# Block sums of a weight tile written over its own blocks, and the scaling of x moved ahead of the weight splits in two engines' queues

## The chip, the cores and the metric

One Trainium2 chip; the kernel runs on one of its cores. The metric is the device time of one execution in microseconds (us). A matmul runs on PE (TensorE); DVE is VectorE, ACT is ScalarE, POOL is GpSimd, SP is the engine whose queue issues most DMAs.

## The reference, cut to what matters

A decoder layer on 256 rows of width 2048 in float32: a feed-forward block, a mixing layer, a second feed-forward block, a final norm. Both feed-forward blocks (hidden width 5632) compute

```python
def swiglu(x, w_gate, w_up, w_down):
    return (jax.nn.silu(x @ w_gate) * (x @ w_up)) @ w_down
h = h + 0.5 * swiglu(rms_norm(h, ffn1_norm[l]), ffn1_w_gate[l], ffn1_w_up[l], ffn1_w_down[l])
```

The change lies in `x @ w_gate` and `x @ w_up` of these two blocks.

## The kernel before, in words

**Split products.** Every float32 operand is held as a high part (fp32r, a CAST by ACT) and a low part (what the cast lost, a subtraction by DVE). A product is three matmuls: high times high, high times low, low times high (`three`, L133 to L138). A weight block can therefore not be used before ACT and then DVE have split it: `split` (L93 to L101, L99 on ACT, L100 on DVE) takes one buffer of tag `whi` and one of `wlo`, of which there are three each, and a buffer comes free when the last matmul that reads it is done.

**Chunks and passes.** The hidden width is cut in a first chunk of 512 columns and five of 1024 (`ffn`, L246 on). The first chunk uses ordinary products (`weights`, `rows_times`; its splits are L81 and L82). Each of the five others is a gate pass and an up pass (L315, L321), so there are 20 passes in the two blocks. A pass goes over eight pairs of 128-row weight tiles, in the order of the plan "nSnSnSnn": `n` is an ordinary pair (two splits of 128x1024, 24 matmuls), `S` is a pair done by a Strassen-like scheme (21 matmuls) on the four 128x512 blocks b11, b12 (upper row) and b21, b22. This text calls the three S pairs of a pass S1, S2 and S3.

**An S pair before the change** (`pairs`, L103 to L131). It needs b11 and b21 (one split of 128x1024), b22 (a split of 128x512), and four sums: t1 = b12 - b11 and t3 = b22 - b12 (L125, one instruction of 128x1024), t2 = t3 + b11 (L127), t4 = b21 - t2 (L128). The sums go to a second `wst` buffer (there are three `wst` buffers in all, 1 MB each, and a DMA from HBM fills one per pair), and are split in turn: t1 with t3, then t2 with t4. So an S pair has four splits: (b11, b21), b22, (t1, t3), (t2, t4). PE takes b21, b11, b22, then t1 and t3, t2, t4 (L156 to L162), and the pair before and after it are ordinary or S by the plan. The splits go round the three buffers, so the buffers of b22 and of (t1, t3) are those that the two halves of the ordinary pair before it gave up.

**What sets the order.** The program is not ordered by hand. A scheduler runs it once against a model when it is built, and each engine's queue is the order in which instructions start there: of those that are ready, the one with the smallest number starts, and that number is the place in the program less an offset. Loads, splits and sums of weights carry an offset of 4000 (L60, L111), all the rest, if nothing is said, none.

**After a pass.** At the last S the partial sums in PSUM are combined (`shared`, L300 to L304, DVE and ACT). After a gate pass DVE adds them to four banks (L317) and ACT takes silu (L318); after an up pass DVE adds and multiplies (L324, L325). The transposes of the hidden values and their split (`hidden_T`, L270 and L271) come at pair 6 of the next gate pass.

**Scaling of x.** The row scale of the norm is known late, so the first gate chunk runs on x without it. While the first up chunk runs, `normalised(p)` (L275 to L292) rescales x in place, pair p of its 16 tiles after PE has read that pair: L279 and L280 add the parts and multiply (DVE), L281 casts (ACT), L282 subtracts (DVE); for the three pairs that the S pairs use, four sums of x (L286 to L289), their cast (L291) and subtraction (L292) follow. The temporary is one for all p, so p + 1 follows p. The first gate pass starts with pair p = 3 (an ordinary one), then S1 with p = 0.

Of the kernel before, what the change touches and what calls it, by code (L numbers as in the profile page):

```python
# [12 lines left out]
F32 = mybir.dt.float32  # L13
F32R = mybir.dt.float32r
AF = mybir.ActivationFunctionType
ALU = mybir.AluOpType
PSUM = bass.MemoryType.PSUM
P = 128
# [3 lines left out]
class Core:  # L22
# [80 lines left out]
    def pairs(self, mat, c0, plan):  # L103


        nc = self.nc
        ns = plan.count("S")
        ids = {"S": iter(range(ns)), "n": iter(range(ns, self.NK // 2))}
        for kind in plan:
            p = next(ids[kind])  # L110
            with self.tc.high_priority(offset=4000):  # L111
                st = self.wpool.tile([P, 2 * self.WMAX], F32, name=self.name("wst"), tag="wst")
                nc.sync.dma_start(
                    out=st.rearrange("p (k f) -> p k f", k=2),
                    in_=mat[2 * p * P : (2 * p + 2) * P, c0 : c0 + 1024].rearrange("(k p) f -> p k f", p=P),
                )
                b = st.rearrange("p (k n f) -> p k n f", k=2, n=2)
                if kind == "n":
                    parts = [self.split(b[:, k], 2) for k in range(2)]
                else:  # L120
                    b11, b21 = self.split(b[:, :, 0, :], 2)
                    (b22,) = self.split(b[:, 1, 1:2, :], 1)
                    tt = self.wpool.tile([P, 2 * self.WMAX], F32, name=self.name("wst"), tag="wst")
                    t = tt.rearrange("p (n f) -> p n f", f=512)
                    nc.vector.tensor_tensor(t[:, 0:2], b[:, :, 1, :], b[:, 0], ALU.subtract)  # L125
                    t1, t3 = self.split(t[:, 0:2], 2)
                    nc.vector.tensor_tensor(t[:, 2], t[:, 1], b[:, 0, 0, :], ALU.add)  # L127
                    nc.vector.tensor_tensor(t[:, 3], b[:, 1, 0, :], t[:, 2], ALU.subtract)  # L128
                    t2, t4 = self.split(t[:, 2:4], 2)
                    parts = dict(b11=b11, b21=b21, b22=b22, t1=t1, t2=t2, t3=t3, t4=t4)  # L130
            yield kind, p, parts  # L131

# [113 lines left out]
def ffn(core, xhi, xlo, rstd, wg, wu, wd, after_first, after_down, fpool, down, rest, back, head=None):  # L246
    nc, NT, NK, D, S = core.nc, core.NT, core.NK, core.D, core.S
# [10 lines left out]
    def hidden_T(c0, w, hid):  # L258
        for j in range(0, w // P, 2):
            bk = core.bank(4 + j // 2)  # L260
            for jj in range(2):
                for t in range(NT):
                    nc.tensor.transpose(  # L263
                        bk[:, jj * 256 + t * P : jj * 256 + (t + 1) * P],
                        hid[:, t, (j + jj) * P : (j + jj + 1) * P],
                        core.ident,
                    )
            k = c0 // P + j
            dst = hT_hi[:, k : k + 2, :].rearrange("p k s -> p (k s)")
            nc.scalar.copy(dst, bk)  # L270
            nc.vector.tensor_tensor(  # L271
                hT_lo[:, k : k + 2, :].rearrange("p k s -> p (k s)"), bk, dst.bitcast(F32), ALU.subtract
            )

    def normalised(p):  # L275

        pair = slice(2 * p, 2 * p + 2)
        tmp = scrap[:, 0, 512:].rearrange("p (k s) -> p k s", k=2)
        nc.vector.tensor_tensor(tmp, xhi[:, pair, :].bitcast(F32), xlo[:, pair, :].bitcast(F32), ALU.add)  # L279
        nc.vector.tensor_tensor(tmp, tmp, core.rb[:, None, :].to_broadcast([P, 2, S]), ALU.mult)  # L280
        nc.scalar.copy(xhi[:, pair, :], tmp)  # L281
        nc.vector.tensor_tensor(xlo[:, pair, :], tmp, xhi[:, pair, :].bitcast(F32), ALU.subtract)  # L282
        if p < NSUM:
            blk = lambda k, t: tmp[:, k, t * P : (t + 1) * P]
            raw = scrap[:, 1, 512:].rearrange("p (n s) -> p n s", n=4)
            nc.vector.tensor_tensor(raw[:, 0], blk(0, 1), blk(1, 1), ALU.add)  # L286
            nc.vector.tensor_tensor(raw[:, 1], raw[:, 0], blk(0, 0), ALU.subtract)
            nc.vector.tensor_tensor(raw[:, 2], blk(0, 0), blk(0, 1), ALU.subtract)
            nc.vector.tensor_tensor(raw[:, 3], blk(1, 0), raw[:, 1], ALU.subtract)  # L289
            flat = raw.rearrange("p n s -> p (n s)")  # L290
            nc.scalar.copy(sums[:, p, 0, :], flat)  # L291
            nc.vector.tensor_tensor(sums[:, p, 1, :], flat, sums[:, p, 0, :].bitcast(F32), ALU.subtract)  # L292

    def blocks_of(dst):
        return [dst[:, t, n * 512 : n * 512 + 512] for t in range(NT) for n in range(2)]

    def shared(aux, dst):

        d11, d12, d21, d22 = blocks_of(dst)
        nc.scalar.copy(d11, aux[0])  # L300
        nc.vector.tensor_tensor(d21, aux[2], d11, ALU.add)
        nc.vector.tensor_tensor(d12, aux[1], d21, ALU.add)
        nc.vector.tensor_tensor(d21, aux[3], d21, ALU.add)
        nc.vector.tensor_tensor(d22, aux[1], d21, ALU.add)  # L304
# [3 lines left out]
    for c0, w in chunks:  # L308
        if c0:
            own, aux = ([core.bank(i) for i in b] for b in (range(4), range(4, 8)))  # L310
            sg = fpool.tile([P, NT, 1024], F32, name=core.name("sg"), tag="sg")
            last_s = GATE_PLAN.rindex("S")
            hooks = {last_s: [lambda: shared(aux, sg)]}
            hooks.setdefault(HIDDEN_AT, []).extend(pending)
            core.rows_times_pairs(wg, c0, GATE_PLAN, own, aux, xhi, xlo, sums, hooks)  # L315
            for d, bk in zip(blocks_of(sg), own):
                nc.vector.tensor_tensor(d, bk, d, ALU.add)  # L317
                core.last_silu = nc.scalar.activation(d, d, AF.Silu)  # L318
            own, aux = ([core.bank(i) for i in b] for b in (range(4, 8), range(4)))
            hid = fpool.tile([P, NT, 1024], F32, name=core.name("hid"), tag="hid")  # L320
            core.rows_times_pairs(wu, c0, UP_PLAN, own, aux, xhi, xlo, sums,  # L321
                                  {UP_PLAN.rindex("S"): [lambda: shared(aux, hid)]})
            for d, g, bk in zip(blocks_of(hid), blocks_of(sg), own):
                nc.vector.tensor_tensor(d, bk, d, ALU.add)  # L324
                nc.vector.tensor_tensor(d, d, g, ALU.mult)  # L325
            pending = [lambda c0=c0, w=w, hid=hid: hidden_T(c0, w, hid)]
            continue
        nb = (w + 511) // 512
        cuts = [(n, n * 512, min(512, w - n * 512)) for n in range(nb)]
        gb = [[core.bank(t * nb + n) for n in range(nb)] for t in range(NT)]  # L330
        for i, (k, hi, lo) in enumerate(core.weights([(wg, c0, w)], ks, head=bool(head))):
            core.rows_times(gb, xhi, xlo, k, hi, lo, w, i == 0, i == NK - 1)
            if head and i in head:
                with core.tc.high_priority(offset=3000), core.tc.issue_after(core.last_mm.ins):
                    head[i]()
        after_first()
        sg = fpool.tile([P, NT, 1024], F32, name=core.name("sg"), tag="sg")
        for t in range(NT):
            for n, c, ww in cuts:
                core.last_silu = nc.scalar.activation(sg[:, t, c : c + ww], gb[t][n][:, :ww], AF.Silu, scale=rstd[:, t : t + 1])  # L340
        ub = [[core.bank(4 + t * nb + n) for n in range(nb)] for t in range(NT)]
        for i, (k, hi, lo) in enumerate(core.weights([(wu, c0, w)], ks)):
            core.rows_times(ub, xhi, xlo, k, hi, lo, w, i == 0, i == NK - 1)
            if i == 0:
                sums, scrap = rest(), sg
            if i % 2:
                normalised(i // 2)
        hid = fpool.tile([P, NT, 1024], F32, name=core.name("hid"), tag="hid")
        for t in range(NT):
            for n, c, ww in cuts:  # L350
                nc.vector.scalar_tensor_tensor(  # L351
                    hid[:, t, c : c + ww], ub[t][n][:, :ww], rstd[:, t : t + 1], sg[:, t, c : c + ww],
                    ALU.mult, ALU.mult,
                )
        pending = [lambda c0=c0, w=w, hid=hid: hidden_T(c0, w, hid)]
# [853 lines left out]
```

## Time and profile before

| | us |
|---|---|
| median of 3 runs (lowest to highest) | 1953.48 (1951.44 to 1953.81) |
| the profiled execution, its own time | 1948.99 |
| its span in the profile | 1947.3 |
| PE busy in the span | 1907.3 (98%) |
| DVE busy | 1440.3 (74%) |
| ACT busy | 985.8 (51%) |
| mean granted clock of PE (1 is full) | 0.994 |

The span is the time from the first to the last instruction that the profile shows. Matmuls are pipelined, and one that takes 0.39 us starts 0.23 us behind the one before it, so a wait of PE of under some 0.16 us does not show in its busy time: PE's waits are read from single rows.

### The profile page before, as it was taken

The page shows a single profiled execution, that of the slowest core. Times are in us where ns is not written, and L with a number is a line of the kernel's source. Part 1 is how long each engine was busy: PE and PEld are TensorE (multiplying, and loading weights), DVE is VectorE, ACT ScalarE, POOL GpSimd, SP SyncE. Part 2 cuts the span into 40 slices and gives each one's busy share as a digit, 9 for nine tenths or more (in the row PEclk, how much of TensorE's full clock was granted, in tenths as well). Part 3 has the DMA queues.
Part 4 walks back from the last instruction along what each step waited for, and adds up shares of the span by engine and source line. Part 5 has one row for each costly group of instructions (what it writes and reads, how often), then busy time and mean ns, then how long its engine had stood idle before and what let it go on. Part 6 is the DMA issues. An engine that isn't in the chain of part 4 may idle for free.

```text
span 1947.3 us, 25669 instructions
## 1 busy us (share of the span) xinstructions
PE 1907.3 (98%) x10233; PEld 1589.7 (82%) x10233; DVE 1440.3 (74%) x1822; ACT 985.8 (51%) x1189; POOL 9.9 (1%) x53
## 2 busy tenths in 40 slices
PE   8899999999999999999999999999999999999997
PEld 6678877878888889998899878778888888788886
DVE  5989898888645446876696775899898989844553
ACT  6465555555444335544454555565556555543443
POOL 0000000000000001000000000000000000000000
PEclk9999999999999999999999999999999999999999
DMA  6356555565755556545243456555555655766553
GB/s 238 129 198 214 173 194 195 178 212 190 264 186 204 194 195 207 177 127 163 77 144 115 131 195 215 173 194 182 199 197 198 211 183 184 257 211 193 195 194 129
DMA packets 130032, 360.77 MB, mean 185 GB/s; under 512 B 20879, under 2 KB 23128, under 8 KB 129784
## 3 DMA queue, kind: packets, MB, share of 16 engines
q1 hardware_dynamic: 129592, 358.08, 55.6%
q8 instruction: 80, 1.31, 0.3%
q10 hardware_dynamic: 320, 1.06, 0.1%
q14 instruction: 40, 0.33, 0.0%
HBM read 351.25 MB, written 7.86 MB: 184 GB/s over the span
## 4 chain that ended last, share of the span: by engine, by line
PE 89%; DVE 5%; ACT 3%; issue 2%; DMA 1%; SPq 0%; ACTq 0%; DVEq 0%
PE bank L137 14%; PE bank L136 13%; PE bank L138 13%; PE bank L175 10%; PE bank L177 10%; PE bank L174 10%; PE bank L186 4%; PE bank L188 4%; PE bank L187 4%; ACT whi L99 1%; DVE wlo L82 1%; PE bank L263 1%; DVE wlo L100 1%; PE bank L712 1%; PE bank L640 1%
## 5 line engine op out<-in xcount | busy, mean ns | idle before, releaser
L82 DVE TENSOR_TENSOR wlo<-wst,whi 128x1024 fp32r<-128x1024 f32 (+2 forms) x329 | 398.2, 1212 | 344.6 <-ACT whi L81 343.9
L99 ACT CAST whi<-wst 128x1024 fp32r<-128x1024 f32 (+1 forms) x440 | 430.4, 993 | 364.0 <-PE bank L138 321.9
L81 ACT CAST whi<-wst 128x1024 fp32r<-128x1024 f32 (+2 forms) x329 | 343.2, 1044 | 472.5 <-PE bank L177 335.8
L100 DVE TENSOR_TENSOR wlo<-wst,whi 128x1024 fp32r<-128x1024 f32 (+1 forms) x440 | 493.3, 1147 | 90.9 <-ACT whi L99 85.0
L174 PE MATMUL bank<-whi,hThi 128*128 128x512 f32 x704 | 274.2, 389 | 0.0
L175 PE MATMUL bank<-wlo,hThi 128*128 128x512 f32 x704 | 274.0, 389 | 0.0
L177 PE MATMUL bank<-whi,hTlo 128*128 128x512 f32 x704 | 231.4, 389 | 0.0
L186 PE MATMUL bank<-xahi,whi 128*128 128x256 f32 x688 | 199.1, 290 | 3.2 <-DVE raw L571 3.2
L188 PE MATMUL bank<-xahi,wlo 128*128 128x256 f32 x688 | 197.9, 288 | 0.0
L136 PE MATMUL bank<-whi,xahi 128*128 128x512 f32 x490 | 191.4, 393 | 6.3 <-ACT xahi L281 4.6
L187 PE MATMUL bank<-xalo,whi 128*128 128x256 f32 x688 | 197.3, 287 | 0.0
L137 PE MATMUL bank<-wlo,xahi 128*128 128x512 f32 x490 | 191.5, 391 | 0.6 <-DVE wlo L100 0.6
L136 PE MATMUL bank<-whi,xbhi 128*128 128x512 f32 x490 | 190.2, 391 | 1.9 <-DVE hid L351 1.4
L137 PE MATMUL bank<-wlo,xbhi 128*128 128x512 f32 x490 | 191.1, 390 | 0.6 <-DVE wlo L100 0.6
L138 PE MATMUL bank<-whi,xalo 128*128 128x512 f32 x490 | 191.4, 391 | 0.0
L138 PE MATMUL bank<-whi,xblo 128*128 128x512 f32 x490 | 190.7, 389 | 0.0
L175 PEld LDWEIGHTS bank<-wlo,hThi 128*128 128x128 f32 x704 | 132.2, 188 | 27.4
L177 PEld LDWEIGHTS bank<-whi,hTlo 128*128 128x128 f32 x704 | 132.1, 188 | 27.4
L174 PEld LDWEIGHTS bank<-whi,hThi 128*128 128x128 f32 x704 | 132.2, 188 | 27.1
L186 PEld LDWEIGHTS bank<-xahi,whi 128*128 128x128 f32 x688 | 133.1, 193 | 7.3 <-DVE raw L571 3.6
L188 PEld LDWEIGHTS bank<-xahi,wlo 128*128 128x128 f32 x688 | 132.9, 193 | 1.9 <-issue 1.1
L187 PEld LDWEIGHTS bank<-xalo,whi 128*128 128x128 f32 x688 | 133.1, 194 | 1.2 <-issue 0.2
(298 smaller groups left out, 2557.3 us busy)
## 6 DMA issues: line engine op xcount, KB each, us to landing
wst<-in_ffn_w_up_dram SPq DMA_DIRECT2D x88, 1024.0 KB, 5.0
wst<-in_ffn_w_down_dram SPq DMA_DIRECT2D x88, 1024.0 KB, 4.9
wst<-in_ffn_w_gate_dram SPq DMA_DIRECT2D x87, 1024.0 KB, 5.0
wst<-in_w_in_dram SPq DMA_DIRECT2D x40, 1024.0 KB, 5.0
wst<-in_w_out_dram SPq DMA_DIRECT2D x16, 1024.0 KB, 5.7
h<-parked SPq DMA_DIRECT2D x4, 1024.0 KB, 9.2
wst<-in_w_in_dram SPq DMA_DIRECT2D x4, 640.0 KB, 4.4
h<-in_x_dram SPq DMA_DIRECT2D x4, 512.0 KB, 4.7
```

Of the source, the lines that this page charges most:

```text
L82: nc.vector.tensor_tensor(lo[:, : m * width], src, hi[:, : m * width].bitcast(F32), ALU.subtract)
L99: self.nc.scalar.copy(hv, src)
L100: self.nc.vector.tensor_tensor(lv, src, hv.bitcast(F32), ALU.subtract)
L136: nc.tensor.matmul(out, a[0], b[0], start=first, stop=False)
L137: nc.tensor.matmul(out, a[0], b[1], start=False, stop=False)
L138: self.last_mm = nc.tensor.matmul(out, a[1], b[0], start=False, stop=last)
L174: nc.tensor.matmul(banks[t][n][:, :w], a, whi[:, c : c + w], start=first, stop=False)
L175: nc.tensor.matmul(banks[t][n][:, :w], a, wlo[:, c : c + w], start=False, stop=False)
L177: self.last_mm = nc.tensor.matmul(banks[t][n][:, :w], b, whi[:, c : c + w], start=False, stop=last)
L186: nc.tensor.matmul(out, a, xhi[:, k, :], start=first, stop=False, skip_group_check=True)
L187: nc.tensor.matmul(out, a, xlo[:, k, :], start=False, stop=False, skip_group_check=True)
L188: nc.tensor.matmul(out, b, xhi[:, k, :], start=False, stop=last, skip_group_check=True)
```

## The change

In `pairs`, the second `wst` buffer goes. The four sums are written over the blocks of the loaded tile: w22 becomes t3, w12 becomes t1, w11 becomes t2, w21 becomes t4, by four instructions of 128x512. A block is overwritten, so its split and every other reader come first. The splits of (t1, t3) and (t2, t4) then read the loaded tile. In `ffn`, `normalised` runs under an offset of 4500.

```diff
                     b11, b21 = self.split(b[:, :, 0, :], 2)
                     (b22,) = self.split(b[:, 1, 1:2, :], 1)
-                    tt = self.wpool.tile([P, 2 * self.WMAX], F32, name=self.name("wst"), tag="wst")
-                    t = tt.rearrange("p (n f) -> p n f", f=512)
-                    nc.vector.tensor_tensor(t[:, 0:2], b[:, :, 1, :], b[:, 0], ALU.subtract)
-                    t1, t3 = self.split(t[:, 0:2], 2)
-                    nc.vector.tensor_tensor(t[:, 2], t[:, 1], b[:, 0, 0, :], ALU.add)
-                    nc.vector.tensor_tensor(t[:, 3], b[:, 1, 0, :], t[:, 2], ALU.subtract)
-                    t2, t4 = self.split(t[:, 2:4], 2)
+
+                    w11, w12, w21, w22 = b[:, 0, 0, :], b[:, 0, 1, :], b[:, 1, 0, :], b[:, 1, 1, :]
+                    nc.vector.tensor_tensor(w22, w22, w12, ALU.subtract)
+                    nc.vector.tensor_tensor(w12, w12, w11, ALU.subtract)
+                    nc.vector.tensor_tensor(w11, w22, w11, ALU.add)
+                    nc.vector.tensor_tensor(w21, w21, w11, ALU.subtract)
+                    t1, t3 = self.split(b[:, :, 1, :], 2)
+                    t2, t4 = self.split(b[:, :, 0, :], 2)
                     parts = dict(b11=b11, b21=b21, b22=b22, t1=t1, t2=t2, t3=t3, t4=t4)
...
             if i % 2:
-                normalised(i // 2)
+                with core.tc.high_priority(offset=4500):
+                    normalised(i // 2)
```

## Rows read from the trace of the kernel before

**Rows 1.** The page: busy time of the engines; the chain that ended last, by engine.

```profile
PE 1907.3 (98%) x10233; PEld 1589.7 (82%) x10233; DVE 1440.3 (74%) x1822; ACT 985.8 (51%) x1189; POOL 9.9 (1%) x53
...
PE 89%; DVE 5%; ACT 3%; issue 2%; DMA 1%; SPq 0%; ACTq 0%; DVEq 0%
```

**Rows 2.** Who waited for whom, whole span: us in total, times, longest us.

```profile
PEld bank L137 <- DVE wlo L100: 18.7, 54, 0.9
...
ACT whi L99 <- DMA wst<-in_ffn_w_gate_dram: 10.0, 13, 1.6
```

**Rows 3.** Timeline at an S2, PE's weight load: start us, us, instruction, idle before.

```profile
316.76 0.19 PEld L137 LDWEIGHTS bank<-wlo,xsums 128*128 128x128 f32 x1 [0.38 <-DVE wlo L100]
```

**Rows 4.** Timeline of ACT at the same S2: casts of b22 and (t1, t3).

```profile
311.63 0.63 ACT L99 CAST whi<-wst 128x512 fp32r<-128x512 f32 x1 [1.64 <-PE bank L138]
314.40 1.05 ACT L99 CAST whi<-wst 128x1024 fp32r<-128x1024 f32 x1 [2.14 <-PE bank L138]
```

**Rows 5.** Timeline of DVE at the same S2: low part of b22, last sum, low part of (t1, t3).

```profile
312.68 0.68 DVE L100 TENSOR_TENSOR wlo<-wst,whi 128x512 fp32r<-128x512 f32 x1
313.28 0.68 DVE L128 TENSOR_TENSOR wst<-wst,wst 128x512 f32<-128x512 f32 x1
315.48 3.72 DVE L100 TENSOR_TENSOR wlo<-wst,whi 128x1024 fp32r<-128x1024 f32 x3 [1.52 <-ACT whi L99]
```

**Rows 6.** Timeline of DVE in the first block's scaling: each waits for the one before.

```profile
69.36 0.69 DVE L282 TENSOR_TENSOR xalo<-sg,xahi 128x512 fp32r<-128x512 f32 x1 [0.68 <-ACT xahi L281]
70.08 0.69 DVE L279 TENSOR_TENSOR sg<-xahi,xalo 128x512 f32<-128x512 f32 x1
70.81 0.69 DVE L280 TENSOR_TENSOR sg<-sg,rb 128x512 f32<-128x512 f32 x1
```

**Rows 7.** Timeline of DVE and ACT between a gate pass and its up pass's S1.

```profile
378.42 1.28 DVE L317 TENSOR_TENSOR sg<-bank,sg 128x512 f32<-128x512 f32 x2
381.34 3.50 DVE L100 TENSOR_TENSOR wlo<-wst,whi 128x1024 fp32r<-128x1024 f32 x3 [1.64 <-ACT whi L99]
...
379.14 1.23 ACT L318 ACTIVATE sg<-sg 128x512 f32<-128x512 f32 x2 [0.78 <-DVE sg L317]
380.28 2.97 ACT L99 CAST whi<-wst 128x1024 fp32r<-128x1024 f32 x3
```

**Rows 8.** Timeline of DVE between an up pass and the next gate pass's S1.

```profile
327.07 1.22 DVE L125 TENSOR_TENSOR wst<-wst 128x1024 f32<-128x1024 f32 x1
328.24 0.69 DVE L324 TENSOR_TENSOR hid<-bank,hid 128x512 f32<-128x512 f32 x1
...
329.98 0.69 DVE L127 TENSOR_TENSOR wst<-wst,wst 128x512 f32<-128x512 f32 x1
...
333.66 0.69 DVE L100 TENSOR_TENSOR wlo<-wst,whi 128x512 fp32r<-128x512 f32 x1
334.27 0.69 DVE L325 TENSOR_TENSOR hid<-hid,sg 128x512 f32<-128x512 f32 x1
334.87 1.28 DVE L324 TENSOR_TENSOR hid<-bank,hid 128x512 f32<-128x512 f32 x2
336.07 1.28 DVE L325 TENSOR_TENSOR hid<-hid,sg 128x512 f32<-128x512 f32 x2
337.27 3.49 DVE L100 TENSOR_TENSOR wlo<-wst,whi 128x1024 fp32r<-128x1024 f32 x3
```

**Rows 9.** Timeline of PE at the first block's first gate pass.

```profile
69.38 0.80 PE L136 MATMUL bank<-whi,xahi 128*128 128x512 f32 x1 [4.56 <-ACT xahi L281]
```

**Rows 10.** Windows: us, busy PE, PEld, DVE, ACT, POOL (instructions), granted clock, DMA, GB/s.

```profile
60.00:70.00 10.00, 3.18 (x11) 1.76 (x10) 9.28 (x16) 3.19 (x5) 0.00 (x0) 0.77 0.33 105
70.00:80.00 10.00, 9.79 (x38) 7.47 (x37) 8.53 (x13) 5.20 (x7) 0.00 (x0) 0.89 0.32 105
...
1250.00:1260.00 10.00, 8.64 (x39) 6.82 (x38) 10.00 (x16) 5.21 (x6) 0.00 (x0) 1.00 0.25 85
1260.00:1270.00 10.00, 8.88 (x35) 6.33 (x35) 8.47 (x13) 4.07 (x6) 0.00 (x0) 1.00 0.44 144
```

## The prediction, made before the changed kernel was seen

> **What bounds the kernel now.** I read the page first: PE is busy for 98% of the span and holds 89% of the chain that ended last, DVE 5%, ACT 3% [rows 1]. So work off PE costs nothing by itself; what counts is where PE stands still. The view of waits tells where, inside the passes: PE's weight loads waited 54 times for a low part of L100, 18.7 us together, while ACT's 13 waits for a gate DMA, at most 1.6 us each, are ACT's alone [rows 2]. The timeline at one S2 shows what that wait is: PE waits 0.38 us for the low part of (t1, t3) [rows 3]. Its cast began when PE gave a buffer back, at 314.40 [rows 4], and DVE, idle for 1.52 us, took the low part up the moment the cast was done, at 315.48 [rows 5]. So the loop PE, ACT, DVE, PE has no slack at (t1, t3): whatever reaches DVE or ACT late there, PE loses. The other place is the start of each block's first gate pass, where DVE is full and PE waits for scaled x: 4.56 us in one wait [rows 9], 6.82 us idle in one window of 10 us, at a granted clock of 0.77 and then 0.89 of full (means of the two levels, 1.2 and 2.4 GHz, over a window); 1.36 and 1.12 us idle in two windows of the second block, at 1.00 [rows 10]. With the clock (0.23 of 3.2 us and 0.11 of 9.8 us of work, at most 1.8) that is some 11 us, and nearly all that the edits could bring: the steady passes have only the short waits above.
>
> **The sums, part by part.** 60 S pairs (20 passes of three) are touched.
>
> *Work.* L125 goes and becomes two instructions of half the width. A step of 512 columns takes 0.60 us from start to start (two of L317 span 1.28, the last of them 0.68 [rows 7]), one of 1024 about 1.17 (327.07 to 328.24 [rows 8]): DVE gains next to nothing. Hidden by DVE's idle quarter [rows 1], zero.
>
> *Buffers and DMAs.* No DMA is added. Loads may use all three `wst` buffers, but an S tile is held until (t2, t4) is split, some 4 us longer. PE is not shown waiting for a load, and the ACT waits are within ACT's idle half: zero. If a load came late after all, its price is at most ACT's 1.6 us.
>
> *The place of the sums.* This is the step that costs. Before, the sums needed the load and nothing else: at the S2 shown the last one starts at 313.28, 2.2 us ahead of the low part of (t1, t3), and nobody waits for it [rows 5]. After it, the first sum overwrites b22 and must come behind b22's split, whose cast ends at 312.26 because its buffer came back from PE only then [rows 4]. From there DVE must do the low part of b22, four sums, and the low part of (t1, t3), one behind the other. The new wait is the first sum's, for ACT's and DVE's halves of that split; behind it on DVE stand the other sums and the low parts of (t1, t3) and (t2, t4), on ACT the cast of (t2, t4) waits for the last sum, and PE for all of them. Each of the first four steps is read or overwritten by the next. Such neighbours start 0.72 us apart (69.36, 70.08, 70.81 [rows 6]), independent ones 0.60 [rows 7]. The low part of (t1, t3) then starts at 312.26 + 0.03 + 4 x 0.72 + 0.60 = 315.77 in place of 315.48: 0.29 us late, and PE with it. The cast of (t1, t3) needs the second sum, done at 312.29 + 2 x 0.72 + 0.68 = 314.41, as late as it now starts. Bounds: if dependent steps cost 0.60, the chain is 0.12 x 4 shorter and nothing is late (0); if the last sum falls behind the low part of (t1, t3), it ends at 315.48 + 1.17 + 0.68 = 317.33, the cast of (t2, t4) follows, and PE waits some 0.7 more. I take 0.29, since rows 6 are the same engine, shape and kind of neighbour. The 40 S2 and S3: **+11.6 us** (0 to +28).
>
> The Trainium skill (VectorE: DVE Perf Modes, The DRAIN you can't avoid) has it that consecutive DVE operations take the same time with a semaphore between each as with one at the end. By it the four gaps of 0.12 would vanish and the +11.6 would be 0; the rows, 0.72 against 0.60, say otherwise. It is a rival below.
>
> *S1 of a gate pass that follows an up pass, 8 times.* DVE must also finish L324 and L325. Before, three slots ahead of b22's low part held sums, and after it five of these operations lay, so that (t1, t3) came at 337.27 [rows 8]. After, L125's slot stays empty (the first L324 cannot start before 328.24), those of L127 and L128 take two of the five, and the other three fall between the sums, where they fill the gaps: 333.66 + 0.60 + 3 x 0.60 + 4 x 0.60 + 0.12 = 338.6, which is 1.3 us late. Bounds: 0.29 (the three go behind the sums) and 2.5 (none moves up: two more steps of 0.60). I take 1.3, since a queue takes what is ready: **+10.4 us**.
>
> *S1 of an up pass, 10 times.* There the cast of (t1, t3) waits behind two silus, and these behind L317 [rows 7]. With the first two sums and two L317 after b22's low part it starts at 378.42 + 4 x 0.60 + 0.12 = 380.94, not 380.28, and the low part after two more sums at 382.3, not 381.34: 0.9 late; 0 if the sums fall into the gaps. I take the middle: **+5 us** (0 to +9).
>
> The two S1 that are left lie in the starts, next.
>
> **The scaling, part by part.** Each of 16 `normalised` issues 4 DVE and 1 ACT instructions (6 of them 9 and 2), and no DMA; they pass the splits L81, L82, L99 and L100 in ACT's and DVE's queues, not in SP's or POOL's. In the first block S1's sums (1.17 + 0.60 + 0.60) and its first split (1.17) need only a load and a buffer, so they can stand ahead of the scaled x that PE waits for at 69.38 [rows 9]; without them PE could start 3.5 us earlier. But DVE was 93% busy while PE waited [rows 10], and the work is put off, not saved: it comes back before S1, with four more scalings. What PE can keep is what DVE then catches up, its 1.47 us of idle time in the next window, and part of the lost clock. The second block has 1.5 us of idle time in the like window. S1's own late sums take some of it back. I take **-3 us** for both starts, with ends -11 (all waits gone) and +3 (scalings ahead of the first up chunk's splits hold PE up there: one split late by the 3.5 us of a scaling, less its lead).
>
> **The sum.** 11.6 + 10.4 + 5 - 3 = +24 us. The profiled execution took 1948.99 us (its span 1947.3); the median of three runs, 1953.48, is 4.5 higher. So 1973.0 by its own time, 1977.5 as a median. One measurement of this kernel tells about 0.2%, 3.9 us, from no change.
>
> **The rivals.**
> - *The starts pay and the late sums hide* (faster). Place: the first gate pass of each block. DVE does the scaling first, and in the passes the sums fit before (t1, t3). It decides where the sums cost PE under 0.12 us per S pair: then 60 times at most 7 us stands against up to 11. For it: 4.56 us in one wait on one cast [rows 9]; 1.52 us of idle DVE right where the sums would go [rows 5]. Against: that idle time is used up to the last 0.3 us by my chain. Price: -11 at best, 1942.5 us; -6 as a middle, 1947.5.
> - *Gains and losses meet* (no change): the chain is free (0.60 between neighbours), S1 costs 0.29 x 18 = 5 us, and the starts give 5 back: 1953.5 us.
> - *The chain is free, but S1 pays in full*: 10.4 + 5 - 3 = +12, 1966 us.
> - *The cast of (t1, t3) waits for all four sums*, if the scheduler takes its interleaved halves for a range that holds w21: it starts at 312.29 + 4 x 0.72 + 0.68 = 315.85, 1.45 us late in each of 60: +87, 2040 us. Against it: the old L127 ran between the two splits of the same buffer without holding the one ahead up.
> - *The scaling does not move*, because its operations become ready late anyway: then the forecast loses its -3, 1980.5 us.
>
> **How the numbers follow.** The forecast with the fifth rival has 0.62, free chain with S1 paid 0.08, the wait for all sums 0.04: slower 0.74. Gains and losses meeting has 0.11, the faster rival 0.15. The forecast's own range: at the foot 11.6, S1 at 0.29 in 18 places (5) and -8 for the starts, +9 or 1962; at the head the middle between the values taken and their upper bounds, 20 + 15 + 7 - 1 = +41 or 1994. For 8 in 10 I go on down to 1951, where gains and losses meet; that leaves out the faster rival and the 2040.
>
> **What would show it.** Right: PE's waits for L100 grow from 18.7 us to some 35 to 45, with waits near 0.7 us at S2 and S3, and over 1 us at a gate pass's S1; the sums stand between b22's low part and that of (t1, t3), 0.72 us apart; the wait of 4.56 us shrinks. Wrong: sums 0.60 apart, or (t1, t3) ahead of the last sums with PE no later; PE's waits at S pairs as before; passes as long as before and a start that is shorter by more than 4 us.

## The result, and the profile after

The changed kernel took 1986.26 us (median of 4 runs, 1985.59 to 1987.99) beside 1952.46 for the kernel before (4 runs): a ratio of 1.0175, 95% interval 1.0158 to 1.0193. That is 33.8 us more, where the prediction had 24 more, and inside its range (1951 to 1994). The profiled execution took 1986.28 us with a span of 1984.3, 37.0 longer than that of before, whose profiled execution lay some 3.5 us under its median.

The page of the changed kernel: busy time of the engines, and the chain that ended last.

```profile
PE 1921.5 (97%) x10233; PEld 1595.2 (80%) x10233; DVE 1469.7 (74%) x1882; ACT 986.7 (50%) x1189; POOL 9.9 (0%) x53
...
PE 73%; DVE 19%; ACT 5%; issue 2%; DMA 0%; ACTq 0%; SPq 0%; DVEq 0%
```

No engine has notably more work: DVE is busy 29 us longer at the same share (a sum lasts 0.69 us, and dependent neighbours start 0.72 apart, where independent ones overlap at 0.60). But its part of the chain went from 5% to 19% [rows 1]: DVE is now what PE waits for, in the main through ACT's casts, while it is no fuller.

Every matmul of a pass stands in the trace, 183 a pass, so a pass can be measured from the start of its first matmul to that of the next pass's first. In the changed kernel the lines from L121 on are moved (sums L125 to L128, matmuls L137 to L139, the ends of passes L318, L319, L325, L326).

| us | before | after | together |
|---|---|---|---|
| up pass (10), mean | 42.42 | 43.31 | +9.0 |
| later gate pass (8), mean | 44.26 | 47.06 | +22.4 |
| up to the end of the first gate pass, block 1 | 113.81 | 117.22 | +3.4 |
| end of block 1's passes to the end of block 2's first gate pass | 802.63 | 804.78 | +2.2 |
| sum | | | +37.0 |

Not all of the last two rows belongs to the change. In block 1, PE is 2.0 us later before anything that was changed has begun (last section). Between the blocks, in the mixing layer, the granted clock was low for longer in the profile of the changed kernel. Here are the windows at the same place in the kernel before and in the changed one (columns as in [rows 10]):

```profile
915.00:925.00 10.00, 10.00 (x144) 9.65 (x141) 5.78 (x9) 5.45 (x10) 0.00 (x0) 0.83 0.35 112
```

```profile
934.00:944.00 10.00, 10.00 (x126) 9.76 (x123) 5.20 (x8) 4.73 (x10) 0.00 (x0) 0.66 0.35 112
```

PE was busy all through the 20 us ahead of it in both profiles, at full clock, so the rows do not tell why. Counted from the end of block 1's passes, the changed kernel is 1.5 us later from there on, as are eight other profiles, by 1.3 to 2.3; that of the kernel before and four others are not. These 3.5 us are nearly what lies between the 37.0 of the two profiles and the 33.8 of the medians. Counted from behind these two places the starts grew by 1.4 and 0.6 us, 2.0 in place of 5.6.

The view of waits of the changed kernel (who waited for whom: us in total, times, longest):

```profile
ACT whi L99 <- DVE wst L126: 135.4, 59, 3.2
...
PEld bank L137 <- ACT whi L99: 49.7, 61, 2.1
...
ACT whi L99 <- DVE wst L128: 30.1, 39, 2.0
...
PEld bank L138 <- DVE wlo L100: 21.6, 35, 1.4
```

The last row answers to [rows 2]: PE's weight loads wait little more for low parts than before (18.7 us). What grew is their wait for casts. The view of waits of the kernel before had for it:

```profile
PEld bank L136 <- ACT whi L99: 14.6, 25, 2.1
```

So 14.6 became 49.7 us, and the two new rows of ACT say why: its casts now wait for sums, that of (t1, t3) for L126 and that of (t2, t4) for L128.

**At an S2**, DVE and then ACT in the timeline of the changed kernel (start us, us, instruction, idle before):

```profile
357.74 0.69 DVE L100 TENSOR_TENSOR wlo<-wst,whi 128x512 fp32r<-128x512 f32 x1 [0.61 <-ACT whi L99]
358.46 0.69 DVE L125 TENSOR_TENSOR wst<-wst 128x512 f32<-128x512 f32 x1
359.19 0.69 DVE L126 TENSOR_TENSOR wst<-wst 128x512 f32<-128x512 f32 x1
359.91 0.69 DVE L127 TENSOR_TENSOR wst<-wst 128x512 f32<-128x512 f32 x1
360.64 0.69 DVE L128 TENSOR_TENSOR wst<-wst 128x512 f32<-128x512 f32 x1
361.25 3.64 DVE L100 TENSOR_TENSOR wlo<-wst,whi 128x1024 fp32r<-128x1024 f32 x3
```

```profile
359.99 1.05 ACT L99 CAST whi<-wst 128x1024 fp32r<-128x1024 f32 x1 [2.29 <-DVE wst L126]
361.44 2.00 ACT L99 CAST whi<-wst 128x1024 fp32r<-128x1024 f32 x2 [0.40 <-DVE wst L128]
```

The sums start 0.72 to 0.73 us apart, and the low part of (t1, t3) starts 3.51 us behind that of b22: the chain that the prediction wrote down (0.72 x 4 + 0.60 = 3.48), to 0.03 us. DVE's idle 1.52 us of [rows 5] is gone. What PE meets is this:

```profile
362.55 0.50 PE L137 MATMUL bank<-whi,xsums 128*128 128x512 f32 x1 [0.29 <-ACT whi L99]
```

PE waits here for the high part of (t2, t4), cast behind the last sum (361.44 + 1.0 = 362.44); the low part of (t1, t3) is done at the same moment (361.25 + 1.22 = 362.47). PE's standstill is counted as the excess of one matmul's start over the 0.227 us to the next: 0.56 us here, 0.23 at an S2 before.

**At S1 of a later gate pass**, DVE, then ACT, then PE in the timeline of the changed kernel:

```profile
344.87 0.69 DVE L100 TENSOR_TENSOR wlo<-wst,whi 128x512 fp32r<-128x512 f32 x1
345.48 0.69 DVE L326 TENSOR_TENSOR hid<-hid,sg 128x512 f32<-128x512 f32 x1
346.08 0.69 DVE L125 TENSOR_TENSOR wst<-wst 128x512 f32<-128x512 f32 x1
346.68 0.69 DVE L325 TENSOR_TENSOR hid<-bank,hid 128x512 f32<-128x512 f32 x1
347.28 0.68 DVE L126 TENSOR_TENSOR wst<-wst 128x512 f32<-128x512 f32 x1
347.88 0.69 DVE L326 TENSOR_TENSOR hid<-hid,sg 128x512 f32<-128x512 f32 x1
348.48 0.69 DVE L127 TENSOR_TENSOR wst<-wst 128x512 f32<-128x512 f32 x1
349.16 1.23 DVE L100 TENSOR_TENSOR wlo<-wst,whi 128x1024 fp32r<-128x1024 f32 x1
350.30 0.68 DVE L128 TENSOR_TENSOR wst<-wst 128x512 f32<-128x512 f32 x1
```

```profile
348.08 1.05 ACT L99 CAST whi<-wst 128x1024 fp32r<-128x1024 f32 x1 [3.24 <-DVE wst L126]
351.10 2.95 ACT L99 CAST whi<-wst 128x1024 fp32r<-128x1024 f32 x3 [1.97 <-DVE wst L128]
```

```profile
349.18 0.73 PE L137 MATMUL bank<-whi,xsums 128*128 128x512 f32 x2 [0.24 <-ACT whi L99]
350.44 0.50 PE L138 MATMUL bank<-wlo,xsums 128*128 128x512 f32 x1 [0.53 <-DVE wlo L100]
352.19 0.50 PE L137 MATMUL bank<-whi,xsums 128*128 128x512 f32 x1 [0.56 <-ACT whi L99]
353.14 0.72 PE L137 MATMUL bank<-whi,xahi 128*128 128x512 f32 x2 [0.21 <-ACT whi L99]
```

Three steps of L325 and L326 fall into the gaps between the dependent sums, as forecast; each makes the distance of two neighbours of the chain 1.20 in place of 0.72. But then the cast of (t1, t3), which needs only L126, is done just before L127 is (348.08 + 1.05 = 349.13 against 348.48 + 0.69 = 349.17): its low part (349.16, 1.23 us) goes **ahead of the last sum**. This order was not chosen while the kernel ran: the queue was fixed when it was built, by the scheduler's model, and the times of the trace agree with that choice. So PE stands twice: 1.32 us for (t1, t3), at 349.18 and 350.44, and another 1.33 us for the cast of (t2, t4) and for what is queued behind it, at 352.19 and 353.14. Before, this S1 cost 0.29 us.

### The profile page after: what moved, and what is told of

Its sections match the earlier page's. It is cut to its first block, busy times and chain, and to the rows that moved or that the text cites. A ratio compares the mean times of both kernels' runs of the same rounds, so it can differ in the third digit from the quotient of the medians.

```text
span 1984.3 us, 25722 instructions
## 1 busy us (share of the span) xinstructions
PE 1921.5 (97%) x10233; PEld 1595.2 (80%) x10233; DVE 1469.7 (74%) x1882; ACT 986.7 (50%) x1189; POOL 9.9 (0%) x53
## 4 chain that ended last, share of the span: by engine, by line
PE 73%; DVE 19%; ACT 5%; issue 2%; DMA 0%; ACTq 0%; SPq 0%; DVEq 0%
PE bank L176 10%; PE bank L178 10%; PE bank L175 10%; PE bank L138 9%; PE bank L139 9%; PE bank L137 8%; DVE wlo L100 5%; ACT whi L99 4%; PE bank L187 4%; PE bank L189 3%; PE bank L188 3%; DVE wst L126 2%; DVE wst L127 2%; DVE wst L125 2%; DVE wst L128 2%
## 5 line engine op out<-in xcount | busy, mean ns | idle before, releaser
L137 PE MATMUL bank<-whi,xahi 128*128 128x512 f32 x490 | 189.6, 394 | 2.7 <-ACT whi L99 2.0
L139 PE MATMUL bank<-whi,xalo 128*128 128x512 f32 x490 | 191.7, 392 | 0.0
L139 PE MATMUL bank<-whi,xblo 128*128 128x512 f32 x490 | 190.9, 390 | 0.0
L137 PE MATMUL bank<-whi,xbhi 128*128 128x512 f32 x490 | 188.4, 391 | 0.9 <-ACT whi L99 0.9
```

The source lines that it names most:

```text
L137: nc.tensor.matmul(out, a[0], b[0], start=first, stop=False)
L139: self.last_mm = nc.tensor.matmul(out, a[1], b[0], start=False, stop=last)
```

## The experiments

Theory: the loss is the late place of the sums, as a chain of dependent DVE steps behind b22's split; S1 of a gate pass loses most, because other DVE work falls in between and the low part of (t1, t3) passes the last sum. Rivals: the scaling's new place; the `wst` buffer held longer; the mere number of steps. Passes are given as up / later gate pass; the changed kernel has 43.31 / 47.06, the one before 42.42 / 44.26. Each ratio is to runs of the kernel before taken beside that run. Recorded expectations name a run by its label, which stands in brackets behind its heading here.

**The two parts of the change, one at a time.** First the changed kernel without the scaling's offset (e1):

```diff
-                with core.tc.high_priority(offset=4500):
-                    normalised(i // 2)
+                normalised(i // 2)
```

> The sums in place, the scaling left where it was. Theory (the sums stand late on the path of the split of (t1, t3), the scaling gives nothing): 1.016 to 1.019 times before, 1984 to 1990 us, with up passes of 43.3 us and later gate passes of 47.1 us as in the changed kernel. Rival (the scaling's move itself costs the 5.6 us by which the two starts grew): about 1.014, 1980 us or less.

1984.88 us, ratio 1.0168 (1.0152 to 1.0183); 43.3 / 47.1. The sums alone make nearly the whole loss. Then the kernel before with that offset alone (e2):

> The scaling moved ahead, the sums as before in a buffer of their own. Theory: passes after the first as before (42.4 and 44.1 us), the starts within 3 us of before, so 0.998 to 1.001. Rival (scaling ahead costs at the starts, since the last operations of the first up chunk come later): 1.002 to 1.004, with the first gate passes longer.

1950.3 us, ratio 0.9995 (0.9986 to 1.0003): no difference that can be told. Yet in block 1 PE has finished S1 of the first gate pass at 78.58 us (81.06 before), and S2 only at 92.21 (91.47 before); in block 2 S1 is 1.7 us earlier and S2 1.8 later, with 1.8 us lost to the clock between the blocks, ahead of both. DVE at that S2 in the timeline of this kernel:

```profile
84.19 0.68 DVE L280 TENSOR_TENSOR sg<-sg,rb 128x512 f32<-128x512 f32 x1
84.79 1.22 DVE L125 TENSOR_TENSOR wst<-wst 128x1024 f32<-128x1024 f32 x1
85.92 0.68 DVE L282 TENSOR_TENSOR xalo<-sg,xahi 128x512 fp32r<-128x512 f32 x1
86.52 0.68 DVE L127 TENSOR_TENSOR wst<-wst,wst 128x512 f32<-128x512 f32 x1
87.19 1.23 DVE L100 TENSOR_TENSOR wlo<-wst,whi 128x1024 fp32r<-128x1024 f32 x1
88.33 0.68 DVE L128 TENSOR_TENSOR wst<-wst,wst 128x512 f32<-128x512 f32 x1
```

Scalings of the last pairs have pushed S2's sums back until the last sum again stands behind the low part of (t1, t3). What S1 wins, S2 gives back.

**The late place without the overwriting.** The kernel before, its three sums queued behind b22's low part, still in a buffer of their own (e3, shown in part; `last_lo` is the low part of the last split):

```diff
+                    with self.tc.issue_after(self.last_lo.ins):
                         nc.vector.tensor_tensor(t[:, 0:2], b[:, :, 1, :], b[:, 0], ALU.subtract)
+                        nc.vector.tensor_tensor(t[:, 2], t[:, 1], b[:, 0, 0, :], ALU.add)
+                        nc.vector.tensor_tensor(t[:, 3], b[:, 1, 0, :], t[:, 2], ALU.subtract)
...
```

> Before, with the three sums (a buffer of their own, scaling not moved) queued on DVE behind the low part of b22. No operand is overwritten; only the place changes. Of these steps just one pair of neighbours depends on each other without an operation between. Theory (place, and 0.12 us per dependent pair): low part of b22, 0.60, first sum 1.26, second 0.72, third 0.60, so the low part of (t1, t3) starts at its old time in S2 and S3: up passes 42.4 to 42.8 us; but the operations of the pass before still fall between the sums at S1 of a gate pass, 1.5 to 2.4 us late: gate passes 45.7 to 46.6; in all 1.007 to 1.011. Rival 1 (overwriting and the longer held buffer are the cause): 1.000. Rival 2 (the place alone costs it all, the gaps nothing): 1.016.

1978.02 us, ratio 1.0132 (1.0118 to 1.0146), above what was expected; 43.7 / 45.6. The gate passes lose 1.3 us, less than in place and a little less than expected; S1 has 0.9 of it (1.5 to 2.4 expected) and S2 0.17. The up passes miss the expectation by more, and at another place: behind S3, where the sums of banks stand in the way. DVE and PE there, in the timeline of this kernel (L302 is L301 of before):

```profile
326.55 0.69 DVE L302 TENSOR_TENSOR hid<-bank,hid 128x512 f32<-128x512 f32 x1 [0.82 <-PE bank L139]
327.15 2.35 DVE L100 TENSOR_TENSOR wlo<-wst,whi 128x1024 fp32r<-128x1024 f32 x2
```

```profile
328.43 0.50 PE L138 MATMUL bank<-wlo,xahi 128*128 128x512 f32 x1 [0.55 <-DVE wlo L100]
```

L302 waits for PE with two low parts queued behind it, and PE then stands 0.71 us for the first of these. So the late place costs where DVE is full even without overwriting, but this run does not give its price alone.

**In place, but earlier.** The changed kernel with t1 and t3 written over w11 and w12, right behind the split of (b11, b21) (e4, shown in part):

```diff
                     b11, b21 = self.split(b[:, :, 0, :], 2)
+                    nc.vector.tensor_tensor(w11, w12, w11, ALU.subtract)
+                    nc.vector.tensor_tensor(w12, w22, w12, ALU.subtract)
                     (b22,) = self.split(b[:, 1, 1:2, :], 1)
...
+                    t1, t3 = self.split(b[:, 0], 2)
+                    nc.vector.tensor_tensor(w22, w22, w11, ALU.subtract)
+                    nc.vector.tensor_tensor(w21, w21, w22, ALU.subtract)
+                    t4, t2 = self.split(b[:, 1], 2)
```

> As the changed kernel, in place and with the scaling ahead, but t1 goes over b11 and t3 over b12, which need only the split of (b11, b21), one buffer earlier; then t2 = b22 - t1 over b22 and t4 = b21 - t2 over b21, both behind the split of b22. Same number of operations, one buffer as in the changed kernel. Theory (the cost is the place of t1 and t3 behind the split of b22): passes near those of before, 42.4 to 42.8 and 44.1 to 45.0 us; 0.998 to 1.004. Rival (sums in place cost by the held buffer or by their number): 1.012 or more.

1964.82 us, ratio 1.0066 (1.0052 to 1.008); 42.35 / 45.67. S2 and S3 stand as short as before (0.23), the up passes are as before: overwriting itself costs nothing there, the place of the first two sums did. The total missed its expectation by the gate passes, where S1 still loses 1.5 us, and by the two first gate passes (53.18 and 49.00). DVE and ACT there, in the timeline of this kernel:

```profile
340.98 1.22 DVE L100 TENSOR_TENSOR wlo<-wst,whi 128x1024 fp32r<-128x1024 f32 x1
342.12 0.69 DVE L128 TENSOR_TENSOR wst<-wst 128x512 f32<-128x512 f32 x1
```

```profile
342.91 2.95 ACT L99 CAST whi<-wst 128x1024 fp32r<-128x1024 f32 x3 [2.24 <-DVE wst L128]
```

Again the low part of (t1, t3) ahead of the last sum, and PE's second standstill: 0.73 + 0.11 + 0.39 + 0.11 us, the same four steps as in the changed kernel.

**The other DVE work taken from between the sums.** The changed kernel, its four products L326 put off to the next gate pass, under an offset of 4500, so ahead of the splits (4000) in DVE's queue (e7, shown in part):

```diff
-                nc.vector.tensor_tensor(d, d, g, ALU.mult)
+            def multiplied(hid=hid, sg=sg, later=c0 + w < DFF):
+                with ExitStack() as behind:
+                    if later:
+                        behind.enter_context(core.tc.issue_after(core.last_lo.ins))
+                        behind.enter_context(core.tc.high_priority(offset=4500))
...
+            products = [multiplied]
```

> The changed kernel, but the four multiplications of an up pass's end (L325 before, L326 after) are issued behind the low parts of the ordinary pair that follows S1, so that three to four steps of 0.60 us no longer fall between the sums of a gate pass's S1. Theory (a gate pass's S1 costs 2.4 us because other DVE work falls between the dependent sums): the eight later gate passes go from 47.07 to 45.0 to 45.9 us, up passes stay at 43.3, the first gate passes stay at 52.7 and 48.0; 1970 to 1978 us, 1.009 to 1.013 of the kernel before. Rival (that S1 is late because of where the sums stand, as S2 and S3 are, whatever lies between): gate passes stay at 46.5 to 47.1, 1982 to 1987 us. Second rival (the work put off is late again at the next S): gate passes gain at S1 and lose at S2, 46 to 47 us.

1977.92 us, ratio 1.0138 (1.0123 to 1.0154); 43.3 / 46.2. S1 of the gate pass now stands for 0.56 us, as an S2 does (2.65 in the changed kernel): its extra loss was the work between the sums. But S2 now stands for 1.79. The products, with their larger offset, lie ahead of b22's low part, and the first sum, which needs it, starts 2 us behind the cast of b22 (done at 352.33):

```profile
350.06 2.49 DVE L339 TENSOR_TENSOR hid<-hid,sg 128x512 f32<-128x512 f32 x4
352.47 1.82 DVE L100 TENSOR_TENSOR wlo<-wst,whi 128x1024 fp32r<-128x1024 f32 x2
354.32 0.69 DVE L125 TENSOR_TENSOR wst<-wst 128x512 f32<-128x512 f32 x1
```

So the mechanism of the first theory and the gate passes of the second rival (46 to 47 us). Whether the products would cost less behind the splits was not tried. The same with the earlier sums (e8):

> The order of sums of e4 (t1 and t3 right behind the split of b11 and b21, t2 and t4 behind that of b22), scaling where it was before, and the four multiplications put off as in e7. Theory (what e4 still costs in a later gate pass, 1.5 us, is the cast of t2 and t4 behind the last sum, and this behind other DVE work): gate passes 44.2 to 44.9 us (e4: 45.67), up passes 42.4, first gate passes as in e4; 1954 to 1960 us, 1.000 to 1.004 of the kernel before. Rival (it is the chain of split, sum, sum, split alone): gate passes 45.4 to 45.7, 1963 to 1966 us.

1959.7 us, ratio 1.004 (1.0027 to 1.0052); 42.4 / 45.3. S1 stands for 0.23 us (0.29 in the kernel before), S2 for 1.44. The gate passes land between the two expectations, for the same reason.

**S1 with a buffer of its own**, S2 and S3 in place (e9): the old lines of `pairs` under `if p == 0`.

> The changed kernel, but S1 of each of the 20 passes has its sums in a buffer of its own, as before; S2 and S3 keep them in place. Theory (0.33 us at each S2 and S3, the rest of the loss at S1): later gate passes 44.6 to 45.0 us (47.07 in the changed kernel, 44.13 before), up passes 42.9 to 43.1 (43.31 and 42.39), first gate passes 1.5 to 3 us shorter than in the changed kernel; 1960 to 1966 us, 1.004 to 1.007 of the kernel before. Rival (what S1 loses comes from the second half of the passes, in that an S3 in place leaves DVE and ACT late for the end of the pass): gate passes stay above 46 us, over 1975 us.

1960.04 us, ratio 1.0047 (1.0034 to 1.0059); 43.0 / 44.7. Time and passes are as the theory says, and the rival is out; only the first gate pass of block 2 is no shorter than in the changed kernel (47.92). S2 and S3 in place, with the scaling ahead, cost 7.4 us of the median.

**The first gate passes with a buffer of their own** (e10): the old lines in the first gate pass of each block only.

> The changed kernel, but the first gate pass of each block (two of the 20) has its sums in a buffer of their own, as before; the scaling stays ahead of the splits. Theory (the starts lose by the late sums, not by the scaling's place): the first gate passes go from 52.7 and 48.0 to 49 to 50.5 and 45.8 to 47.6 us, all other passes as in the changed kernel; 1981 to 1985 us, 1.014 to 1.0165 of the kernel before. Rival (the starts lose because the scaling holds up the first splits): first gate passes stay at 52 to 53 and 48, 1986 us. If the scaling brought the 3 us forecast and only the sums took it back, the two first gate passes with the stretch ahead of them come out 3 us shorter than in the kernel before, 7 to 8 us less than in the changed kernel, 1978 to 1980 us.

1981.5 us, ratio 1.0154 (1.0141 to 1.0168); the two first gate passes 49.31 and 47.54. These lie in the ranges of the theory, but the first pass of block 1 also starts later here, so its length alone says too much. The growth against the kernel before, up to the end of the first gate pass, is counted in block 1 from the first matmul that reads `rdiag`, some 20 us ahead of that pass, and in block 2 from that block's first matmul, so that the two stretches of low clock are left out (one profiled execution each):

| us | block 1 | block 2 |
|---|---|---|
| sums in place alone (e1) | +2.47 | +0.29 |
| scaling ahead alone (e2) | +0.93 | +0.20 |
| the changed kernel | +1.43 | +0.59 |
| the same, first gate passes with a buffer of their own (e10) | +0.75 | +0.17 |

The late sums make 0.7 and 0.4 us of what the starts lose in the changed kernel; without them the starts are still no shorter than before, so the third case of the expectation, a gain of 3 us from the scaling, is out. The two parts do not add up: with the sums in place, the scaling ahead takes 1.0 us off block 1.

**One more step in the chain** (e13).

```diff
                     nc.vector.tensor_tensor(w12, w12, w11, ALU.subtract)
+                    nc.vector.tensor_tensor(w11, w11, w11, ALU.max)
```

> The changed kernel with one more dependent step of 128x512 between the second and the third sum of each S pair (w11 becomes the larger of itself and itself, so no value changes). Theory (PE stands at the end of the chain of dependent steps at every S pair, and each step costs 0.72 us of it): 0.72 us more at each S2 and S3 and at S1 of an up pass, at least as much at S1 of a gate pass; up passes from 43.31 to 45.3 to 45.6 us, later gate passes from 47.07 to 49.0 to 49.6; some 42 to 46 us more, 2027 to 2033 us, 1.038 to 1.041 of the kernel before. Rival (DVE's idle time takes part of it, PE being held by something else, such as ACT's cast behind the second sum): up passes under 44.5 us, less than 25 us more, under 2012 us.

2063.23 us, ratio 1.0568 (1.0554 to 1.0583); 47.3 / 51.0. Neither: 77 us more than the changed kernel, 1.33 at each S of an up pass in place of 0.72. The lines of DVE at an S2 (L128 and L129 are the last two sums here):

```profile
334.17 0.69 DVE L128 TENSOR_TENSOR wst<-wst 128x512 f32<-128x512 f32 x1
334.78 1.22 DVE L100 TENSOR_TENSOR wlo<-wst,whi 128x1024 fp32r<-128x1024 f32 x1
335.92 0.68 DVE L129 TENSOR_TENSOR wst<-wst 128x512 f32<-128x512 f32 x1
```

The low part of (t1, t3) stays where it was and PE stands 0.43 us for it; the last sum has fallen behind it, and PE stands 1.33 us more for the cast of (t2, t4). The price of a step here is a jump. In the changed kernel's S2 the last sum starts 0.40 us before the cast of (t1, t3) is done (360.64 against 359.99 + 1.05): a step of 0.72 more turns the order. By the same sum one filler between the last two sums would, as it puts the last one off by 1.20 - 0.72 = 0.48.

**A better place for the scaling.** Since the scalings of the last pairs spoilt S2 in the run with scaling alone, the kernel before with the offset on the first pairs only (e11):

```diff
-                normalised(i // 2)
+                with core.tc.high_priority(offset=4500 if i // 2 <= 4 else 0):
+                    normalised(i // 2)
```

> The kernel before (sums in a buffer of their own), with the offset of 4500 on the scaling of pairs 0 to 4 alone; pairs 5 to 7 stay without. In e2, with the offset on all eight, the first gate pass was 2.5 us ahead of the kernel before at the end of S1 and 0.7 us behind at the end of S2, where scalings of the last pairs stood between the sums. Theory (what S2 loses in e2 is these scalings): S2's waits go, the first gate passes with the stretch ahead of them are 1 to 2.5 us shorter than in the kernel before, the rest as before; 1948 to 1951.5 us, 0.998 to 1.000 of the kernel before. Rival (the work put off is late wherever it stands: it comes at S3 or as a wait for scaled x of pairs 5 to 7): no gain, 1952 to 1954 us.

1946.58 us, ratio 0.9971 (0.9959 to 0.9982), a little below the expected range. S2 loses next to nothing any more, and the first gate passes take 46.31 and 43.80 us (50.77 and 45.80 before); counted with the stretch ahead, as in the table above, they end 2.2 and 3.6 us earlier. With pairs 0 to 3 (e12):

> As e11, with the offset on pairs 0 to 3 alone (the ordinary pair at the head of the first gate pass needs pair 3, its S1 needs pair 0; pair 4 is read next). Theory: S1 as early as in e2, S2 without its waits, 1 to 2.5 us shorter per block than the kernel before; 1948 to 1951.5 us. Rival (pair 4 is then late for the second ordinary pair): a wait for scaled x of 1 to 3 us behind S1, 1952 to 1956 us.

1946.28 us, ratio 0.9971 (0.9959 to 0.9983): pair 4 is not late. In both, the first up pass of block 2 is 2.6 and 3.1 us longer, with this row of PE in the first of them:

```profile
1305.92 0.50 PE L136 MATMUL bank<-whi,xbhi 128*128 128x512 f32 x1 [1.65 <-DVE sg L303]
```

L303 frees banks at the end of the gate pass; it came late behind scalings of the last pairs. With pairs 0 to 5 (e14):

> As e11, with the offset on pairs 0 to 5. In e11 and e12 S2 of the first gate pass lost nothing, but in the second block the scaling of pairs 5 to 7 was done only at the end of the gate pass, the sums of banks after it (L303) came late, and the first up pass lost 2.6 to 3.1 us. Theory (those two us are the scaling of the last pairs, late): with pair 5 ahead as well the first up pass of the second block goes from 45.03 to 42.4 to 43.5 us and S2 of the first gate pass still has no waits over 0.3 us; 1943.5 to 1946 us, 0.9955 to 0.998 of the kernel before. Rival (the work of pair 5 falls between the sums of S2, as in e2): S2 loses 1 to 3 us, 1946.5 to 1949 us.

1945.51 us, ratio 0.9973 (0.9961 to 0.9984). That up pass is 42.51 us and S2 has no waits: the cause was right, though the ratio shows no gain over pairs 0 to 4. In its timeline (1942.12 us, the fastest of seven runs) PE has one wait left between 40 and 118 us:

```profile
64.73 0.79 PE L136 MATMUL bank<-whi,xahi 128*128 128x512 f32 x1 [3.92 <-ACT xahi L281]
```

All three are faster than both kernels of this study, by some 6 us (0.3%) and some 40 us.

## Why the prediction was right, and where it was not

The direction was right for the reason given: the sums, once late, stand between two splits on DVE, and PE waits behind them. Term by term, from the two profiled executions:

| term | predicted | measured |
|---|---|---|
| S2 and S3 | +11.6 | +10.3 |
| S1 of a gate pass, 8 times | +10.4 | +18.9 |
| S1 of an up pass, 10 times | +5 | +2.8 |
| starts | -3 | +5.6 |
| sum | +24 | +37.6 |

Read from single rows, the terms add up to a little more than the 37.0 of whole passes.

*S2 and S3.* 0.29 us each was forecast. Up passes show 0.38 at S2 and 0.31 at S3, gate passes 0.33 at S2 and some 0.1 at S3 (0.31, of which 0.2 comes back in the next pair, the one with the transposes); with 10 and 8 passes that is 10.3, the four S pairs of the first gate passes being counted in the starts. The taken value of the gap, 0.72 [rows 6], was the right one. The Trainium skill (VectorE: DVE Perf Modes, The DRAIN you can't avoid), which the prediction weighed, found no extra time for a semaphore behind each of eight `tensor_copy`. The sums of the changed kernel start 0.72 to 0.73 apart, so for dependent `tensor_tensor` steps here the measurement decides against carrying that over. What failed is the mark by which it was to be seen: it was the waits for casts that grew, and not those for low parts, because the cast of (t2, t4) is done within 0.03 us of the low part of (t1, t3).

*S1 of a gate pass.* This is the step that was mis-sized. Its working foresaw the three fillers between the sums, and the wait for (t1, t3) grew by 1.32 - 0.29 = 1.03 us, against 1.3 forecast. But it had the low part of (t1, t3) behind all four sums. The last sum was overtaken, and the wait of 1.33 us for (t2, t4) was in no term: the overtaking stood only as an upper bound at S2 and S3, at 0.7 us, and was never carried over to S1, where the fillers make it happen. 2.36 x 8 = 18.9. It is luck in part that the time still lay inside the range: its upper end allowed 20 us for an overtaking at S2 and S3, which did not come there, and 15 for this term.

*S1 of an up pass.* 0.28 us in place of 0.5, between the bounds: PE stands for 0.62 us there, about as long as at S2.

*Starts.* The forecast had the wrong sign. 3.5 of the 5.6 us lie where the change touches nothing: 2.0 ahead of the scaling in block 1 and 1.5 between the blocks. Of the rest, +2.0, a gain is there: by the end of the first ordinary pair PE is 2.5 and 3.3 us earlier than before, and the single wait of 4.56 us [rows 9] is gone. Either part of the change brings most of it alone (the sums 1.7 and 3.3, the scaling 1.9 and 2.9). But S1 of the first gate passes loses 2.4 and 2.3 us, as much as S1 of a later gate pass, now with scalings as the fillers; in block 1 most of it is one wait for the cast of (t2, t4):

```profile
80.19 0.50 PE L137 MATMUL bank<-whi,xsums 128*128 128x512 f32 x1 [1.67 <-ACT whi L99]
```

The ordinary pair behind it and S2 together lose another 1.5 us in each block. The prediction gave these late sums no number of their own, only "some of it". With the scaling alone PE is still 2.5 us earlier at the end of S1 in block 1. The sentence that the work "comes back before S1" had the place wrong: it came back at S2, and in full.

*Rivals.* That the starts pay and the late sums hide, and that gains and losses meet, fall with the sums' 0.72 and with 0.9995 for the scaling alone. The cast of (t1, t3) waits for two sums, not four, so the 2040 is out: the row of L126 in the waits.

*Slips.* Two slips of the working changed little. A scaling has three DVE instructions (L279, L280, L282), eight with the sums of x, where four and nine were counted. And the middle of -3 and +3 is 0, not -1, so the upper end of the range would be 1995.

What stays open: why the scaling ahead helps block 1 when the sums are in place and not when they are early. The overtaking was shown by making it happen and by taking the fillers away; forcing the last sum ahead of the low part in S1 was not tried.

## What to carry to other kernels

Before an in-place update frees a buffer, ask whose last read it now has to follow: an operation that could run as soon as its data had arrived becomes a link between two steps that were already in step with the bound engine. Price such a chain by the start-to-start time of dependent neighbours, and then ask at each join which of two instructions will be ready first, since one slot more can turn their order and cost more than its own length. Work that is moved ahead is not saved: move only so much of it as the next deadline needs, as the scaling of the first pairs did.

## What the runs showed of the hardware that was not expected

The gap between DVE neighbours is the same when the second only overwrites what the first has read, as the prediction took it to be: L126 writes w12, which L125 reads and does not write, and starts 0.73 us behind it (358.46 to 359.19), where independent steps of this size start 0.60 apart (345.48 to 346.08).

PE's granted clock fell in stretches that the change does not touch, and not in every profile. One lies between the blocks (the section on the result). The other comes near the start. The windows of 20 to 30 us of the kernel before and of the changed one (columns as in [rows 10]):

```profile
20.00:30.00 10.00, 9.46 (x40) 7.54 (x41) 5.95 (x5) 4.65 (x5) 0.00 (x0) 1.00 0.59 190
```

```profile
20.00:30.00 10.00, 9.08 (x32) 7.09 (x33) 5.06 (x5) 4.33 (x5) 0.00 (x0) 0.83 0.44 123
```

The mean 0.83 lies between the two levels, 1.2 and 2.4 GHz. Four of the fourteen profiles (the two kernels and the twelve runs) show it, those of the changed kernel, of the earlier sums with products put off, of the first gate passes with a buffer of their own, and of the scaling of pairs 0 to 4; in these four the matmuls that read `rdiag`, some 20 us before the first gate pass, start at 40.8 to 41.1 us, in the other ten at 38.2 to 39.4. In the 10 us ahead of it PE was busy for 8.5 us in the changed kernel and for 8.1 in the one before, so the rows do not tell what set it off.
